# One exponential, product and store for a pair of heads, with accumulators, residual rows and the sample tile moved in a Mamba-2 and latent-attention step

## The chip, the cores and the metric

The kernel runs on one core of a Trainium2 chip. A core has four compute engines that this text calls by their names in the profile: PE (TensorE, the matrix unit), DVE (VectorE), ACT (ScalarE) and POOL (GpSimd). SP (SyncE) computes nothing and issues transfers. Each engine runs its own list of instructions in order, and engines wait for one another by semaphores. SBUF is the on-chip memory with 128 partitions, PSUM the accumulators that PE writes and DVE and ACT read. Transfers are issued from SP's, ACT's or POOL's queue.

The metric is the device time of one launch in microseconds (us), lower is better. Before the change it is 1969.66 us as the median of three runs (1962.78 to 1971.03).

## The reference

One inference step of two layers: a Mamba-2 layer, then a multi-head latent attention layer (MLA). There are 1024 prompt tokens, and eight sequences of eight sample tokens that attend to 2048 cached positions in pages of 128. All of it is in float32. What the change touches is the MLA layer and the final normalisation:

```python
def latent_partial(q_lat, q_pe, ckv, kpe, mask):
    s = (jnp.einsum('bqhc,bkc->bhqk', q_lat, ckv.astype(F32))
         + jnp.einsum('bqhr,bkr->bhqk', q_pe.astype(F32), kpe.astype(F32))) * MLA_SCALE
    if mask is not None:
        s = jnp.where(mask, s, NEG_INF)
    m = jnp.max(s, axis=-1)
    p = jnp.exp(s - m[..., None])
    return m, jnp.sum(p, axis=-1), jnp.einsum('bhqk,bkc->bhqc', p, ckv.astype(F32))
...
def latent_out(l, acc, w_uv):
    return jnp.einsum('bhqc,chv->bqhv', acc / l[..., None], w_uv.astype(F32))
...
def mla_sample_attn(q_nope, q_pe, ckv, kpe, pool_ckv, pool_kpe, layer, page_table, w_uk, w_uv):
...
    stats = latent_partial(q_lat, q_pe, ckv, kpe, causal)
    def page_step(carry, pt):
        page = latent_partial(q_lat, q_pe, pool_ckv[layer, pt], pool_kpe[layer, pt], None)
        return merge_partial(carry, page), None
    (_, l, acc), _ = lax.scan(page_step, stats, page_table.T)
    return latent_out(l, acc, w_uv)

def mla_output(o, gate, w_out):
    b, t = o.shape[:2]
    gated = o.reshape(b, t, MLA_WIDTH) * jax.nn.silu(gate.astype(F32))
    return jnp.einsum('bte,ed->btd', gated.astype(gate.dtype), w_out)
...
        hp = hp + out_p.astype(hp.dtype)
        hs = hs + out_s.astype(hs.dtype)
    y_prompt = rms_norm(hp, final_norm_w)
    y_sample = rms_norm(hs, final_norm_w)
```

There are 16 heads with 64 output columns each, the latent rows have 256 columns, and the model width is 1024.

## The kernel before

**Precision.** A float32 product is made of three matmuls on rounded halves: each operand is split into a high part (`split`, line 128, a copy on ACT) and a low part (line 129, a subtraction on DVE or POOL), and high x high, high x low and low x high are added up in PSUM.

**Stages.** The Mamba-2 layer takes the first half of the time. The MLA layer (`layer_mla`, line 2427) then projects, and runs the prompt's 16 heads one after the other (`mla_heads`, line 1932). The sample's attention over the cached pages is begun within the last two heads and goes on behind them (`mla_sample`, line 2314), with the prompt's output projection laid between its steps.

**Order.** In heads 0 to 13 PE and POOL run in the order of the program text, and a scheduler sorts the other engines' instructions. From head 14 on (`sm.begin`) all engines run in the order of the text.

**A prompt head.** Twelve steps, four for the first 512 queries (qc=0) and eight for the second (qc=1), one for each block of 128 keys. `hd.qk` issues three score matmuls, on the diagonal a fourth for the mask, two exponentials on ACT (th, line 1873, and P, line 1874), and their difference tl (line 1876) on POOL, or on DVE for each fourth block. `hd.pv` runs three steps later: three matmuls into the accumulator `o` (lines 1901 to 1903, one PSUM buffer); at the same time it loads the next gates. Units of work for the coming heads stand between the steps: maxima (`maxpass`, with the matmul nmp on line 1845 that waits for DVE's nm, line 1842), projections, and from head 14 the sample's.

**A head's end.** Behind the last block of a (head, qc), ACT takes the logarithm of the row sums (line 1912), DVE multiplies output and gate into `og` (line 1913), and ACT turns the logarithm into a reciprocal (line 1914). Three steps later, `close` (line 1916) multiplies the two on POOL (line 1917) and stores them to `og_d` in DRAM (line 1918), by SP's queue, and from head 14 by POOL's. Head h uses partitions 64j to 64j+63 with j = h mod 2, so each of the 32 pieces has 64 partitions x 512.

**The sample's start.** `sm.begin` at the start of head 14 makes `nk96`, the new tokens' rotary keys in three parts, with four DVE operations (lines 2051 to 2054). `sm.prefetch` is run as four units of head 14, the first two close together. Each loads a page group by an indirect transfer from POOL (line 2105); the second also transposes `nk96` on PE (line 2071, nkp) and copies it back (line 2072).

**The sample's steps.** `flow` (line 2269) goes over 32 items, four page groups for each of eight sequences. Step n transposes and splits the latent rows of item n+1 (key casts on line 2188, subtractions on 2190), computes the scores of item n, its running maximum (line 2122), and the exponential P (line 2132), and turns P by transposes (pt, line 2219) one step later to multiply it with the latent rows (o). When a sequence has its four items, `turn_acc` (line 2244) transposes its accumulator on PE (act, line 2250) and copies it into accT on DVE (line 2251). In the program before it runs in the step with n mod 4 = 1, right behind `first_acc`, which copies the next sequence's first accumulator on ACT (ac, line 2170).

**The output projection.** `MlaOut.pieces` (line 2346) handles tiles of 128 tokens in four pieces of 12 matmuls each (line 99 in `mm_tok`), one piece for each step of `flow` from step 5 on. At a tile's start the previous tile is closed, the residual rows h are loaded (line 2372), and the next tile's og is loaded. Behind each half of 512 columns DVE adds the product to h (line 2387); behind half 0 the next tile's og is split; behind half 1 ACT squares both halves and sums them (line 2402). The squares' scratch tile has the tag of the og tile, with one buffer for both. `close` (line 2403) makes the scale with two small DVE operations and a power on POOL (line 2407), and scales both halves (line 2414) and stores each (line 2417).

**The tail.** When the items are done, a string says what comes next: p is a piece of the prompt's last tile, a is `turn_acc` of sequence 7, f is `finish` (for eight pairs of heads two matmuls, lo, line 2259, and two DVE products with the gates into gs, line 2266) and starts the sample's output tile, s is a piece of that tile. The sample tile of 64 tokens stores its rows from two queues (lines 2419 and 2420).

```python
TAIL = "papfpssssspp"
```

Of the kernel before, what the change touches and what calls it, by code (L numbers as in the profile page):

```python
# [17 lines left out]
D = 1024  # L18
# [56 lines left out]
    return nc.sync  # L75


TAIL = "papfpssssspp"
PB1 = {"tr": 2, "pj": 2, "cb": 1, "y": 1, "pv": 1, "st": 1}
PB2 = {"tr": 3, "pj": 2, "y": 3}  # L80
PB = dict(PB1)
# [1527 lines left out]
class Heads:  # L1609
# [55 lines left out]
    def open(self, st, right, psum):  # L1665
        k, tc, nc, I = self.k, self.k.tc, self.k.nc, self.k.I
        self.psum = psum
        top = right.enter_context(open_pool(tc, name="kq3", bufs=1, side="right"))
        self.add_k(top, 2)
        self.add_q(top, 2)  # L1670
        sp = self.sp = st.enter_context(open_pool(tc, name="sp3", bufs=1, side="right"))
        self.add_k(sp, 3)
        for a, b in self.kT:
            nc.gpsimd.memset(a[96:98].bitcast(F32), 1.0)
            nc.gpsimd.memset(b[96:98].bitcast(F32), 0.0)
        self.add_v(sp, 1)
        self.load_mask()
        self.load_q(1)
        self.load_gates(0, 0)

    def load_gates(self, h, qc):
        k, pj = self.k, slice(64 * (h % 2), 64 * (h % 2) + 64)
# [203 lines left out]
    def pv(self, h, qc, jb, th, tl):  # L1886
# [20 lines left out]
        pl = slice(64 - 64 * j, 128 - 64 * j)  # L1907
        cs = slice(512 * qc, 512 * qc + 512)
        gt = self.gt
        og = sp.tile([128, 512], F32, tag="og", name=f"og{h}{qc}", bufs=2)  # L1910
        rl = sp.tile([128, 512], F32, tag="rl", name=f"rl{h}_{qc}", bufs=2)
        nc.scalar.activation(rl[pj], po[pl], AF.Ln)
        nc.vector.tensor_tensor(og[pj], po[pj], gt[pj], op=ALU.mult)
        nc.scalar.activation(rl[pj], rl[pj], AF.Exp, scale=-1.0)

        def close():
            nc.gpsimd.tensor_tensor(og[pj], og[pj], rl[pj], op=ALU.mult)
            (nc.gpsimd if h >= MH - 2 else nc.sync).dma_start(k.og_d[pr, pj, cs], og[pj])
        return close


# [109 lines left out]
class Sample:  # L2031
# [8 lines left out]
    def begin(self, st, hd):  # L2040
        k, nc = self.k, self.k.nc
        self.psum, self.out, self.tags = hd.psum, None, {"tr": ("sc", HB[1]), "sc4": ("sc", HB[1]), "on": ("sc", HB[1])}
        sp = self.ep = self.sp = st.enter_context(open_pool(k.tc, name="ep4", bufs=1))
        pp = st.enter_context(open_pool(k.tc, name="pre4", bufs=1))
        self.w5 = dict(zip(WORD, ([pp.tile([128, D], F32R, name=f"w5p{x}") for x in "hl"], hd.kT[2], hd.qT[2], hd.kT[0])))
        self.smk = sp.tile([128, NT], F32, name="smk")
        nc.sync.dma_start(self.smk, k.I["c_smask"])
        self.load_cn(0)
        nk96 = sp.tile([64, 96], F32, name="nk96")
        rnd = sp.tile([64, 32], F32R, name="nkr")  # L2050
        nc.vector.tensor_copy(rnd, k.nkp)
        nc.vector.tensor_copy(nk96[:, 0:32], rnd.bitcast(F32))
        nc.vector.tensor_tensor(nk96[:, 32:64], k.nkp, rnd.bitcast(F32), op=ALU.subtract)
        nc.vector.tensor_copy(nk96[:, 64:96], rnd.bitcast(F32))
        self.nks, self.nk96 = sp.tile([96, 64], F32R, name="nks"), nk96

    def pt(self, tag, name):
        tag, bufs = self.tags[tag]
# [4 lines left out]
        self.k.nc.sync.dma_start(self.cn, self.k.cs_d[b * NT : b * NT + NT])  # L2063

    def prefetch(self):
        nc = self.k.nc
        for n in range(PRE):
            if n == 1:
                self.load_tk(0)
                p = self.pt("tr", "nkp4")  # L2070
                nc.tensor.transpose(p[:96, :64], self.nk96, self.k.ident[:64, :64])
                nc.vector.tensor_copy(self.nks, p[:96, :64])
                load_halves(self.k, self.w5[WORD[0]], WORD[0])
            self.load(n)
            yield
# [174 lines left out]
            nc.tensor.transpose(pt[:, c * 128 : c * 128 + 128], ac[:, c * 128 : c * 128 + 128], k.ident)  # L2250
        nc.vector.tensor_copy(self.accT[:, :, b], pt[:, :256].rearrange("p (c e) -> p c e", c=2))

    def finish(self):
        k, nc, sp, I = self.k, self.k.nc, self.sp, self.k.I
        gs = self.gs
        for pr in range(8):
            p = self.pt("tr", f"lo{pr}")
            for c in range(2):
                nc.tensor.matmul(p[:, :128].rearrange("p (b e) -> p b e", b=NB),
# [9 lines left out]
    def flow(self):  # L2269
        k, N = self.k, len(self.items)  # L2270
        for n in range(-1, N + 1):
# [8 lines left out]
            if t:  # L2280
                self.turn(n + 1, 1)
                yield
            if n % 4 == 1 and n > 4:
                self.turn_acc(n // 4 - 1)
            if n % 4 == 3 and t:
                self.first_scores(n // 4 + 1)
# [27 lines left out]
def mla_sample(k, sm, st):  # L2314
# [8 lines left out]
    for x in TAIL:  # L2323
        if x == "a":
            sm.turn_acc(NB - 1)
        elif x == "f":
            last = out.pieces((8,), sm.finish())
        else:
            next(last if x == "s" else fill, None)
    drain(fill)  # L2330
# [3 lines left out]
class MlaOut:  # L2334
# [11 lines left out]
    def pieces(self, tiles, src=None):  # L2346
        k, nc, sp, ws = self.k, self.k.nc, self.sp, self.ws

        def load(i):
# [4 lines left out]
            if i < 8:  # L2354
                g = sp.tile([128, 8, 128], F32, tag="og5", name=f"og5{i}", bufs=1)
                nc.sync.dma_start(g, k.og_d[:, :, t0 : t0 + m].rearrange("b p t -> p b t"))
            return oh[:, :, :m], oh[:, :, 64:] if m == 64 else ol, g, oh

        queue = [load(tiles[0])]
        if tiles[0] == 0:  # L2360
# [5 lines left out]
        for n, i in enumerate(tiles):  # L2366
            t0, m = TILES[i]
            if close:
                close()
            oh, ol, _, o2 = queue.pop(0)  # L2370
            h = sp.tile([128, D], F32, tag="h5", name=f"h5{i}", bufs=3)
            nc.sync.dma_start(h[:m], k.h_d[t0 : t0 + m])
            if n + 1 < len(tiles):
                queue.append(load(tiles[n + 1]))
            ss = sp.tile([128, 4], F32, tag="ss5", name=f"ss5{i}", bufs=2)
# [3 lines left out]
            for hf, c in enumerate(cs):  # L2379
# [15 lines left out]
                if hf == 0:  # L2395
                    if n + 1 < len(tiles):
                        split(k, *queue[0][:3])
                if c.stop < D:
                    yield
            if not src:  # L2400
                for hf, c in enumerate(cs):
                    nc.scalar.activation(junk[:, c], h[:m, c], AF.Square, accum_out=ss[:m, hf : hf + 1])
            def close(m=m, h=h, ss=ss, O=O, cs=cs):
                r = ss[:m, 3:4]
                nc.vector.tensor_tensor(r, ss[:m, 0:1], ss[:m, len(cs) - 1 : len(cs)], op=ALU.add)
# [124 lines left out]
```

## Time and profile before

| what | number |
|---|---|
| median of three runs | 1969.66 us (1962.78, 1969.66, 1971.03) |
| the profiled execution | 1961.5 us, span 1959.7 us |
| mean clock granted to PE | 0.987 of full speed |
| instructions | 33894 |
| heads stage, first to last product with the reciprocal | 1361.7 to 1692.9 us |
| last matmul begins | 1949.73 us |
| DMA, whole span | 223.79 MB, mean 114 GB/s |

The span runs from the first to the last recorded instruction of one execution, and the execution's own time has 1.8 us around it. The profile gives each engine's busy time; TensorE's granted clock, as a share of full speed, for any window; the waits, named by the waiting tile with its line, and by what released it; and the chain of work that ended last. A row of the timeline has the start, the duration, the engine, the line, the operation with its output and inputs, and in brackets the idle time of the engine before it with what ended it. The lines themselves stand in the prediction.

### The profile page before, as it was taken

What the parts mean: (1) busy time and instruction counts of PE and PEld (TensorE: products, weight loads), DVE (VectorE), ACT (ScalarE), POOL (GpSimd) and SP (SyncE); (2) the same over time, 40 slices, a digit from 0 to 9 for tenths busy, and PEclk for the clock granted to TensorE, in tenths of its full rate; (3) what the DMA queues carried; (4) which work ended last, traced back from release to release, by engine and by line L of the source; (5) the groups of instructions that cost most, each with busy time, mean ns of one, the idle gap of its engine ahead of it and who ended that gap; (6) DMA issues with size and microseconds to landing.
All of it is one profiled execution on the core that took longest, in us unless ns stands there. A gap on an engine that the chain in (4) does not pass through costs nothing.

```text
span 1959.7 us, 33894 instructions
## 1 busy us (share of the span) xinstructions
PE 1887.0 (96%) x11953; PEld 1732.7 (88%) x11953; DVE 1165.8 (59%) x2566; ACT 1105.8 (56%) x2605; POOL 789.0 (40%) x1094
## 2 busy tenths in 40 slices
PE   7999999999999999799999999999999999899997
PEld 6999999999999999687787998898888887788886
DVE  5457575757575757544425325476777776656664
ACT  5556666666666666643334424335777776655551
POOL 2037373736363657233000001103564556744540
PEclk9999999999999999899999999999999999999999
DMA  5123333233333332644554772232121112854542
GB/s 152 53 61 92 92 89 93 89 92 89 92 89 91 91 89 80 207 153 158 186 181 133 265 281 78 68 108 71 51 70 41 48 45 85 278 150 132 151 128 66
DMA packets 193936, 223.79 MB, mean 114 GB/s; under 512 B 20284, under 2 KB 155336, under 8 KB 193384
## 3 DMA queue, kind: packets, MB, share of 16 engines
q1 hardware_dynamic: 188744, 202.10, 33.9%
q0 software_dynamic: 4944, 19.40, 3.1%
q8 instruction: 95, 1.56, 0.3%
q14 instruction: 73, 0.60, 0.1%
q10 hardware_dynamic: 80, 0.13, 0.0%
HBM read 159.89 MB, written 61.54 MB: 113 GB/s over the span
## 4 chain that ended last, share of the span: by engine, by line
PE 87%; DMA 5%; DVE 3%; ACT 3%; issue 1%; SPq 0%; POOL 0%; ACTq 0%; DVEq 0%; POOLq 0%
PE pj L87 24%; PE pj L99 9%; PE pq L99 6%; PE p L99 4%; PE poa L99 4%; PE pob L99 4%; PE py L863 3%; PE sc L87 2%; PE o L87 2%; PE sc L1830 2%; PE st L1862 2%; PE o L1903 1%; PE st L1863 1%; PE st L1864 1%; PE o L1902 1%; PE o L1901 1%
## 5 line engine op out<-in xcount | busy, mean ns | idle before, releaser
L87 PE MATMUL pj<-xh,wih 128*128 128x384 f32 (+1 forms) x768 | 255.1, 332 | 0.0
L87 PE MATMUL pj<-xh,wil 128*128 128x384 f32 (+1 forms) x768 | 250.8, 327 | 0.0
L87 PE MATMUL pj<-xl,wih 128*128 128x384 f32 (+1 forms) x768 | 250.4, 326 | 0.0
L1876 POOL TENSOR_TENSOR tl<-P,th 128x384 fp32r<-128x384 f32 (+1 forms) x144 | 131.5, 920 | 140.2 <-ACT P L1874 104.7
L129 DVE TENSOR_TENSOR wil<-wraw,wih 128x512 fp32r<-128x512 f32 x92 | 70.4, 765 | 172.6 <-ACT wih L128 172.6
L87 PEld LDWEIGHTS pj<-xh,wih 128*128 128x128 f32 x768 | 144.5, 188 | 0.2
L87 PEld LDWEIGHTS pj<-xl,wih 128*128 128x128 f32 x768 | 144.4, 188 | 0.3
L87 PEld LDWEIGHTS pj<-xh,wil 128*128 128x128 f32 x768 | 144.1, 188 | 0.0
L900 POOL TENSOR_TENSOR y<-y,xD 128x256 f32<-128x256 f32 x64 | 83.9, 1311 | 149.4 <-DVE y L899 138.5
L99 PE MATMUL pj<-wih,xh 128*128 128x256 f32 x504 | 143.3, 288 | 0.0
L99 PE MATMUL pj<-wil,xh 128*128 128x256 f32 (+1 forms) x504 | 139.2, 282 | 0.0
L1873 ACT ACTIVATE th<-st 128x512 fp32r<-128x512 f32 x192 | 94.3, 491 | 69.4 <-PE st L1869 46.7
L2190 POOL TENSOR_TENSOR kvl<-pgr,kvh 128x256 fp32r<-128x256 f32 x128 | 92.2, 748 | 96.3 <-ACT kvh L2188 96.2
L495 DVE SCALAR_TENSOR_TENSOR acc<-raw,vec,acc 128x1112 f32<-128x1112 f32 x84 | 130.5, 1554 | 0.2
L99 PE MATMUL pj<-wih,xl 128*128 128x256 f32 x448 | 126.6, 283 | 0.0
L129 POOL TENSOR_TENSOR xddl<-xdd,xddh 128x256 fp32r<-128x256 f32 x64 | 63.1, 986 | 119.5 <-ACT xddh L128 119.5
L128 ACT CAST Ch<-acc 128x128 fp32r<-128x128 f32 x56 | 16.9, 302 | 153.0 <-PE py L87 153.0
L99 PEld LDWEIGHTS pj<-wih,xh 128*128 128x128 f32 x504 | 96.0, 191 | 0.0
L1874 ACT ACTIVATE P<-st 128x512 f32<-128x512 f32 x192 | 93.4, 486 | 4.3 <-POOL tl L1876 4.0
L99 PEld LDWEIGHTS pj<-wil,xh 128*128 128x128 f32 (+1 forms) x504 | 93.0, 185 | 0.6
L838 ACT ACTIVATE M<-M,tok 128x128 f32<-128x128 f32 (+1 forms) x288 | 90.5, 388 | 1.8 <-DMA M<-acs_d 1.8
L99 PEld LDWEIGHTS pj<-wih,xl 128*128 128x128 f32 x448 | 85.4, 191 | 0.0
(995 smaller groups left out, 6210.4 us busy)
## 6 DMA issues: line engine op xcount, KB each, us to landing
wraw<-in_ssd_w_in SPq DMA_DIRECT2D x92, 256.0 KB
M<-acs_d SPq DMA_DIRECT2D x64, 256.0 KB
y_d<-xD SPq DMA_DIRECT2D x64, 128.0 KB
s<-in_state_ssm SPq DMA_DIRECT2D x32, 256.0 KB
out_s_ssm<-s SPq DMA_DIRECT2D x32, 256.0 KB
wraw<-in_ssd_w_out SPq DMA_DIRECT2D x16, 512.0 KB
q_d<-qt SPq DMA_DIRECT2D x32, 192.0 KB
qp<-q_d SPq DMA_DIRECT2D x8, 768.0 KB
```

The source lines that it names most:

```text
L87: nc.tensor.matmul(out, a, b, start=(i == 0), stop=(i == n - 1))
L99: nc.tensor.matmul(o, a, b, start=(j == 0), stop=(j == len(ops) - 1))
L129: (eng or nc.vector).tensor_tensor(lo, src, hi.bitcast(F32), op=ALU.subtract)
L495: nc.vector.scalar_tensor_tensor(acc, self.raw[bi][:, j : j + n], k.convw[j][:, blk : blk + 1], acc, op0=ALU.mult, op1=ALU.add)
L838: nc.scalar.activation(M[:m, h, :m], M[:m, h, :m], AF.Relu, bias=c.tk[:, 0, 4 * g + h : 4 * g + h + 1], scale=-1.0)
L863: nc.tensor.matmul(py[:m, h * 64 : h * 64 + 64], c.M[:m, h, :m], c.xdt[:m, h * 64 : h * 64 + 64], start=True, stop=True)
L900: nc.gpsimd.tensor_tensor(y[:m], y[:m], c.xD[:m], op=ALU.add)
L1830: nc.tensor.matmul(ps[:, :n], qh[:96, 128 * i : 128 * i + 128], kh[:96, 512 * c : 512 * c + n], start=True, stop=True)
L1873: nc.scalar.activation(th[:, :n], ps[:, :n], AF.Exp, scale=SCALE)
L1874: nc.scalar.activation(P[:, :n], ps[:, :n], AF.Exp, scale=SCALE)
L1876: eng.tensor_tensor(tl[:, :n], P[:, :n], th[:, :n].bitcast(F32), op=ALU.subtract)
L2190: nc.gpsimd.tensor_tensor(rl[:, r], raw[:, r], rh[:, r].bitcast(F32), op=ALU.subtract)
```

## The change

1. The pair's tiles. `og` and `rl` are four fixed tiles of 128 x 512, one of each for a qc. Each head still takes its own logarithm and gate product on its 64 partitions. The even head then ends; the odd head does one exponential, and three steps later one product and one store over both halves. The store goes by POOL's queue for head 15 only.
2. `nk96` is made in the first unit of `prefetch` instead of in `begin`.
3. `turn_acc` runs in the step with n mod 4 = 2 instead of 1.
4. The residual rows h are loaded in `load`, along with the og of the same tile, so a tile ahead.
5. Each half's square follows its own half: half 0's right behind the split of the next tile's og, half 1's at the end.
6. `finish` takes a list of pairs and is called twice, f for pairs 0 to 3 and g for pairs 4 to 7 with the start of the sample's tile, and in the tail all prompt pieces come ahead of the sample's.

```diff
--- before.py
+++ after.py
@@ -75,7 +75,7 @@
     return nc.sync
 
 
-TAIL = "papfpssssspp"
+TAIL = "papfpgpssss"
 PB1 = {"tr": 2, "pj": 2, "cb": 1, "y": 1, "pv": 1, "st": 1}
 PB2 = {"tr": 3, "pj": 2, "y": 3}
 PB = dict(PB1)
@@ -1677,6 +1677,7 @@
         self.load_mask()
         self.load_q(1)
         self.load_gates(0, 0)
+        self.ogs, self.rls = ([sp.tile([128, 512], F32, name=f"{x}{qc}") for qc in range(2)] for x in ("og", "rl"))
 
     def load_gates(self, h, qc):
         k, pj = self.k, slice(64 * (h % 2), 64 * (h % 2) + 64)
@@ -1907,15 +1908,16 @@
         pl = slice(64 - 64 * j, 128 - 64 * j)
         cs = slice(512 * qc, 512 * qc + 512)
         gt = self.gt
-        og = sp.tile([128, 512], F32, tag="og", name=f"og{h}{qc}", bufs=2)
-        rl = sp.tile([128, 512], F32, tag="rl", name=f"rl{h}_{qc}", bufs=2)
+        og, rl = self.ogs[qc], self.rls[qc]
         nc.scalar.activation(rl[pj], po[pl], AF.Ln)
         nc.vector.tensor_tensor(og[pj], po[pj], gt[pj], op=ALU.mult)
-        nc.scalar.activation(rl[pj], rl[pj], AF.Exp, scale=-1.0)
+        if j == 0:
+            return
+        nc.scalar.activation(rl, rl, AF.Exp, scale=-1.0)
 
         def close():
-            nc.gpsimd.tensor_tensor(og[pj], og[pj], rl[pj], op=ALU.mult)
-            (nc.gpsimd if h >= MH - 2 else nc.sync).dma_start(k.og_d[pr, pj, cs], og[pj])
+            nc.gpsimd.tensor_tensor(og, og, rl, op=ALU.mult)
+            (nc.gpsimd if h == MH - 1 else nc.sync).dma_start(k.og_d[pr, :, cs], og)
         return close
 
 
@@ -2046,13 +2048,9 @@
         self.smk = sp.tile([128, NT], F32, name="smk")
         nc.sync.dma_start(self.smk, k.I["c_smask"])
         self.load_cn(0)
-        nk96 = sp.tile([64, 96], F32, name="nk96")
-        rnd = sp.tile([64, 32], F32R, name="nkr")
-        nc.vector.tensor_copy(rnd, k.nkp)
-        nc.vector.tensor_copy(nk96[:, 0:32], rnd.bitcast(F32))
-        nc.vector.tensor_tensor(nk96[:, 32:64], k.nkp, rnd.bitcast(F32), op=ALU.subtract)
-        nc.vector.tensor_copy(nk96[:, 64:96], rnd.bitcast(F32))
-        self.nks, self.nk96 = sp.tile([96, 64], F32R, name="nks"), nk96
+        self.nk96 = sp.tile([64, 96], F32, name="nk96")
+        self.nkr = sp.tile([64, 32], F32R, name="nkr")
+        self.nks = sp.tile([96, 64], F32R, name="nks")
 
     def pt(self, tag, name):
         tag, bufs = self.tags[tag]
@@ -2063,8 +2061,13 @@
         self.k.nc.sync.dma_start(self.cn, self.k.cs_d[b * NT : b * NT + NT])
 
     def prefetch(self):
-        nc = self.k.nc
+        nc, nkp = self.k.nc, self.k.nkp
         for n in range(PRE):
+            if n == 0:
+                nc.vector.tensor_copy(self.nkr, nkp)
+                for j in (0, 2):
+                    nc.vector.tensor_copy(self.nk96[:, 32 * j : 32 * j + 32], self.nkr.bitcast(F32))
+                nc.vector.tensor_tensor(self.nk96[:, 32:64], nkp, self.nkr.bitcast(F32), op=ALU.subtract)
             if n == 1:
                 self.load_tk(0)
                 p = self.pt("tr", "nkp4")
@@ -2250,10 +2253,10 @@
             nc.tensor.transpose(pt[:, c * 128 : c * 128 + 128], ac[:, c * 128 : c * 128 + 128], k.ident)
         nc.vector.tensor_copy(self.accT[:, :, b], pt[:, :256].rearrange("p (c e) -> p c e", c=2))
 
-    def finish(self):
+    def finish(self, pairs):
         k, nc, sp, I = self.k, self.k.nc, self.sp, self.k.I
         gs = self.gs
-        for pr in range(8):
+        for pr in pairs:
             p = self.pt("tr", f"lo{pr}")
             for c in range(2):
                 nc.tensor.matmul(p[:, :128].rearrange("p (b e) -> p b e", b=NB),
@@ -2280,7 +2283,7 @@
             if t:
                 self.turn(n + 1, 1)
                 yield
-            if n % 4 == 1 and n > 4:
+            if n % 4 == 2 and n > 4:
                 self.turn_acc(n // 4 - 1)
             if n % 4 == 3 and t:
                 self.first_scores(n // 4 + 1)
@@ -2324,7 +2327,9 @@
         if x == "a":
             sm.turn_acc(NB - 1)
         elif x == "f":
-            last = out.pieces((8,), sm.finish())
+            sm.finish(range(4))
+        elif x == "g":
+            last = out.pieces((8,), sm.finish(range(4, 8)))
         else:
             next(last if x == "s" else fill, None)
     drain(fill)
@@ -2354,7 +2359,9 @@
             if i < 8:
                 g = sp.tile([128, 8, 128], F32, tag="og5", name=f"og5{i}", bufs=1)
                 nc.sync.dma_start(g, k.og_d[:, :, t0 : t0 + m].rearrange("b p t -> p b t"))
-            return oh[:, :, :m], oh[:, :, 64:] if m == 64 else ol, g, oh
+            h = sp.tile([128, D], F32, tag="h5", name=f"h5{i}", bufs=3)
+            nc.sync.dma_start(h[:m], k.h_d[t0 : t0 + m])
+            return oh[:, :, :m], oh[:, :, 64:] if m == 64 else ol, g, oh, h
 
         queue = [load(tiles[0])]
         if tiles[0] == 0:
@@ -2367,9 +2374,7 @@
             t0, m = TILES[i]
             if close:
                 close()
-            oh, ol, _, o2 = queue.pop(0)
-            h = sp.tile([128, D], F32, tag="h5", name=f"h5{i}", bufs=3)
-            nc.sync.dma_start(h[:m], k.h_d[t0 : t0 + m])
+            oh, ol, _, o2, h = queue.pop(0)
             if n + 1 < len(tiles):
                 queue.append(load(tiles[n + 1]))
             ss = sp.tile([128, 4], F32, tag="ss5", name=f"ss5{i}", bufs=2)
@@ -2395,11 +2400,10 @@
                 if hf == 0:
                     if n + 1 < len(tiles):
                         split(k, *queue[0][:3])
+                if not src:
+                    nc.scalar.activation(junk[:, c], h[:m, c], AF.Square, accum_out=ss[:m, hf : hf + 1])
                 if c.stop < D:
                     yield
-            if not src:
-                for hf, c in enumerate(cs):
-                    nc.scalar.activation(junk[:, c], h[:m, c], AF.Square, accum_out=ss[:m, hf : hf + 1])
             def close(m=m, h=h, ss=ss, O=O, cs=cs):
                 r = ss[:m, 3:4]
                 nc.vector.tensor_tensor(r, ss[:m, 0:1], ss[:m, len(cs) - 1 : len(cs)], op=ALU.add)
```

## The prediction

> **What bounds the kernel now.** First the page: busy times, then the shares of the chain of waits that ended last.
>
> ```profile
> PE 1887.0 (96%) x11953; PEld 1732.7 (88%) x11953; DVE 1165.8 (59%) x2566; ACT 1105.8 (56%) x2605; POOL 789.0 (40%) x1094
> PE 87%; DMA 5%; DVE 3%; ACT 3%; issue 1%; SPq 0%; POOL 0%; ACTq 0%; DVEq 0%; POOLq 0%
> ```
>
> TensorE is busy 96% of the span and carries 87% of the chain, so work taken off ACT, POOL or SP is worth something only where TensorE waits for it. Before 1340 us the change touches nothing. Next comes the view of TensorE's waits from there on, asked in four stretches; columns: total us, count, longest.
>
> ```profile
> PE nmp L1845 <- DVE nm L1842: 2.7, 4, 1.0
> PE o L1903 <- POOL tl L1876: 3.8, 1, 3.8
> PE act L2250 <- ACT ac L2170: 4.1, 7, 1.6
> PE lo L2259 <- DVE gs L2266: 3.1, 1, 3.1
> ```
>
> These are the waits that the change can reach. Last the view by windows: a steady stretch of the heads, then the stretches around three of these waits.
>
> ```profile
> core 0: us, PE busy (x) PEld busy (x) DVE busy (x) ACT busy (x) POOL busy (x), PEclk, DMA share, GB/s
> 1600.00:1640.00 40.00, 39.01 (x227) 33.99 (x226) 31.43 (x82) 31.20 (x69) 23.03 (x27) 1.00 0.12 28
> 1652.80:1656.60 3.80, 0.05 (x1) 0.00 (x0) 0.42 (x1) 0.01 (x1) 2.56 (x3) 0.80 0.07 18
> 1656.60:1662.10 5.50, 5.49 (x17) 4.71 (x18) 1.41 (x4) 1.59 (x5) 5.17 (x6) 0.52 0.28 63
> 1709.80:1713.20 3.40, 3.35 (x9) 2.77 (x10) 2.53 (x5) 0.47 (x1) 2.71 (x3) 0.51 1.03 412
> 1930.30:1933.40 3.10, 0.02 (x1) 0.00 (x1) 1.13 (x4) 0.00 (x0) 0.00 (x0) 1.00 0.29 91
> 1933.40:1938.40 5.00, 4.97 (x23) 4.42 (x24) 3.72 (x15) 0.62 (x1) 0.00 (x0) 0.66 0.00 0
> ```
>
> The heads run at 39.01 of 40 us with the clock at 1.00: 1 us in 40 can be had there. The long waits cost twice: the wait itself, and a stretch behind it at a clock of 0.51 to 0.66, in which a matmul takes about twice as long.
>
> **Change part by part.** *Exponential, product and store per pair.*
>
> ```profile
> L1914 ACT ACTIVATE rl<-rl x32: 621/629/636, 1358.3 to 1689.4; 64x512 f32<-64x512 f32 x32
> L1917 POOL TENSOR_TENSOR og<-og,rl x32: 1259/1278/1603, 1361.7 to 1692.9; 64x512 f32<-64x512 f32 x32
> ```
>
> (Rows grouped by operation: shortest, mean and longest in ns, first and last start.) No row shows these operations on 128 partitions; DVE's products take 0.69 for 64x512 and for 128x512 alike (L1913 and L2387 below), so I take the same for 128 as for 64; at the other bound, twice, nothing would be saved and nothing lost. So 16 x 0.63 = 10 us leave ACT, 16 x 1.28 = 20 us leave POOL, and 16 stores leave the queues (the rest are twice as large). Over 330 us of heads all of it lies behind TensorE's 39 of 40: 0. If that cover were gone it would be a gain, not a loss. What counts is one place, on POOL (timeline: start, us, engine, line, operation; in brackets the idle time before and what ended it):
>
> ```profile
> 1646.66 1.00 POOL L2105 DMA_INDIRECT pgr<-in_cache_ckv,ptidx  x1 [0.30 <-PE o L1902]
> ...
> 1653.96 1.26 POOL L1917 TENSOR_TENSOR og<-og,rl 64x512 f32<-64x512 f32 x1 [4.96 <-DMA pgr<-in_cache_ckv,ptidx]
> ```
>
> The product of head 13 sat 4.96 us behind the landing of page loads that it doesn't use. The subtraction queued behind it on POOL is the one that TensorE waits for (3.8). In the program built from the change, the product waits for the store that last read its tile, for DVE and for ACT, all long done. It then starts at about 1649.0, ends at 1650.3, and the subtraction (1.30) at 1651.6, before TensorE asks at 1652.8. Gain: the 3.8 us, and the half clock behind it, where 5.5 us at 0.52 hold work worth 5.5 x 0.52 = 2.9, so 2.6. I take -6.2; the bounds are 0, if something else holds POOL there, and -6.4.
>
> Two later stalls should shrink, as POOL has a product less in front of them:
>
> ```profile
> 1685.26 0.39 PE L87 MATMUL o<-kvh,pTl 128*128 128x256 f32 x1 [0.94 <-DVE pTl L129]
> ...
> 1695.27 0.66 PE L2219 MATMUL pt<-ident,P 128*128 128x128 f32 x4 [1.40 <-ACT P L2132]
> ```
>
> From 0 to all but 0.6 of their 2.3: I take -0.8.
>
> *The new page's key rows (nk96) moved to prefetch.* Four small DVE operations leave the start of head 14, where they stood ahead of the maximum that a matmul awaits (nmp, longest 1.0). The three other waits of this kind make (2.7 - 1.0) / 3 = 0.6 each and stay, so the gain lies between 0.4 and 1.0; I take -0.7. The operations now stand on DVE behind head 13's gate product, directly ahead of their transposes, whose place on TensorE hasn't moved:
>
> ```profile
> 1636.07 0.85 DVE L2051 CAST nkr<-nkp 64x32 fp32r<-64x32 f32 x1
> 1637.65 0.17 DVE L2053 TENSOR_TENSOR nk<-nkp,nkr 64x32 f32<-64x32 f32 x1
> ...
> 1642.67 0.59 ACT L1912 ACTIVATE rl<-o 64x512 f32<-64x512 f32 x1
> 1642.90 0.26 PE L2071 MATMUL nkp<-ident,nk 64*96 64x64 f32 x1
> 1643.30 0.69 DVE L1913 TENSOR_TENSOR og<-o,gt 64x512 f32<-64x512 f32 x1 [0.26 <-ACT rl L1912]
> ```
>
> TensorE comes to the transpose at 1642.90; the gate product, which waits for the logarithm, ends at 1643.99; four operations at 0.17 make it 1644.7, at 0.85 each 1647.4. So this is a new wait of 1.8 to 4.5 us, with all scores of head 14 behind it in TensorE's queue. POOL is idle then, so the short ones are nearer: +2.0. Waits of 0.94 and 1.40 us had full clock behind them, the one of 1.6 (act, below) had 0.51: a stretch like 1709.80 to 1713.20 costs 3.4 x 0.49 = 1.7, and I count somewhat under half, +0.7. [...]
>
> *Accumulator turned a step later.*
>
> ```profile
> 1709.85 0.69 PE L2250 MATMUL act<-ident,ac 128*128 128x128 f32 x2 [1.56 <-ACT ac L2170]
> 1742.38 0.44 PE L2250 MATMUL act<-ident,ac 128*128 128x128 f32 x2 [0.43 <-ACT ac L2170]
> ```
>
> In the program before, the transpose shares a PSUM buffer with the next batch's first accumulator and waits for ACT's copy issued just ahead. A page step later that copy is some 7 us old; what is left is DVE's copy out of the step before, done by then. 1.56 + 6 x 0.43 = 4.1, and the half clock from 1709.8, 3.4 x 0.49 = 1.7, of which I take 1.4: -5.5 (at least -2.6, if a wait of 0.2 stays in each and the clock still drops; at most -5.8).
>
> *Squares.* Rows of the timeline in the page loop; that of pt is from the chain of waits.
>
> ```profile
> 1723.15 1.03 ACT L128 CAST oh<-og 128x1024 fp32r<-128x1024 f32 x1
> 1724.22 1.22 DVE L129 TENSOR_TENSOR ol<-og,oh 128x1024 fp32r<-128x1024 f32 x1 [0.20 <-ACT oh L128]
> 1729.87 0.69 ACT L2132 ACTIVATE P<-sc,nm 128x512 f32<-128x512 f32 x1 [0.65 <-DVE nm L2125]
> 1733.06 0.44 PE pt L2219 x4
> 1738.33 0.63 ACT L2402 ACTIVATE sq<-h 128x512 f32<-128x512 f32 x1
> 1743.45 0.41 DVE L2251 COPY accT<-act 128x256 f32<-128x256 f32 x1
> ```
>
> Half 0's Square now follows the split of the next tile's outputs. Its scratch tile shares a buffer with the rows that DVE subtracts there, so ACT stands 1.22 for it and 0.63 for the Square, 1.85 in all, once a tile, with the exponential P and the key cast queued behind. P is ready at 1730.56 and its transposes run at 1733.06: 2.5 us of slack, so 0. At the tile's end one Square less: 0.
>
> *Residual rows a tile ahead.* TensorE has no wait on h before the tail, SP issues it behind the next tile's outputs instead of ahead of them, and neither is waited for there: 0.
>
> *Tail.* The sample tile goes last, and its second half of pairs finishes later, so the wait of 3.1 (lo for gs) goes, and with it the half clock at 0.66: 5.0 x 0.34 = 1.7; together -4.8. What is late instead (the first row is from the chain of waits):
>
> ```profile
> 1927.03 5.08 DMA h<-h_d
> ...
> 1937.38 0.69 DVE L129 TENSOR_TENSOR oh<-gs,oh 128x512 fp32r<-128x512 f32 x1 [0.73 <-ACT oh L128]
> 1939.78 0.40 PE L99 MATMUL p<-w5ph,oh 128*128 128x512 f32 x1
> 1943.64 0.68 DVE L2387 TENSOR_TENSOR h<-h,p 64x512 f32<-64x512 f32 x1 [5.56 <-PE p L99]
> 1951.90 0.58 ACTq L2419 DMA_DIRECT2D out_y_sample<-h  x1
> 1951.92 0.69 DVE L2387 TENSOR_TENSOR h<-h,p 128x512 f32<-128x512 f32 x1
> 1954.40 0.55 POOL L2407 TENSOR_TENSOR ss<-ss,nhalf 128x1 f32<-128x1 f32 x1 [3.29 <-DVE ss L2406]
> 1954.99 1.41 DVE L2414 SCALAR_TENSOR_TENSOR h<-h,ss,fw 128x512 f32<-128x512 f32 x2 [0.75 <-POOL ss L2407]
> ```
>
> In DVE's order the split of the sample's outputs (0.69) now stands behind the whole close of tile 7: add 0.69, Square 0.63, the power on POOL 0.55, two scalings 1.41, with the hand-overs 4.7 from the last prompt matmul (about 1937.75) to the sample's first (1942.45). That is +4.7. The half clock behind it costs 1.5 to 2.6. The sample's own chain from its first add to its store's issue, 1951.90 - 1943.64 = 8.3 us, ends the kernel in place of a prompt tile's shorter one. Its h load, queued behind tile 7's two stores, is issued at about 1942.4 and with 5.08 lands 1 us before its use. I get the last store issued at 1956.8 and the end at 1960.0, against 1959.7: +0.3 net (-0.6 to +1.3).
>
> Sum: -6.2 - 0.8 - 0.7 + 2.0 + 0.7 - 5.5 + 0.3 = -10.2. The span of 1959.7 becomes 1949.5, and the profiled 1961.5 (1.8 around the span) 1951.3. The median of the runs shown is 8.2 above that execution, while the lowest run, 1962.78, agrees with it; I set the sum on the mean of all four, 1966.2: **1956**.
>
> **Rivals.** *R1, the gain of the long wait is given back.* From 1692 on the DMA engines are full (share 1.03 in the row at 1709.80): weights and pages then land no earlier however soon POOL is done, and the 6.2 returns as waits for data. For it: that row. Against it: TensorE's waits of 1.4 and 1.6 there name ACT, not a transfer. -4 to -5: 1962.
>
> *R2, slower: ACT's wait in the split.* If P is later than its slack of 2.5, each of the seven tiles pays. It decides from 2.5 us of lateness: the 1.85 above, and whatever DVE's subtraction is late because the accumulator's copy (0.41) now falls into the same step. With the slack used up, 7 x (2.1 + 0.4) = 17 us, and 3 more if half clock follows some: -10 + 17 = +7, up to +10, 1973 to 1976. For it: every n mod 4 = 2 step gains both. Against it: 1.85 + 0.41 is still under 2.5.
>
> *R3, a larger gain.* The nkp wait has no half clock behind it, both later stalls vanish and the tail's wait is shorter than 4.7: -14, 1952. For it: full clock behind 1.40.
>
> *R4, the change doesn't do what it says:* the product still waits for POOL's loads: -10.2 + 6.2 = -4, the same time as R1 and counted with it.
>
> **How the numbers follow.** Forecast 0.54, R3 0.16, R1 with R4 0.20, R2 0.10. Some 0.5% (9.8 us) is what a measurement can tell from nothing. The forecast's spread, 3 us either way, puts 0.31 of its 0.54 beyond it; with R3 0.16 and 0.02 of R1, faster is 0.49. Of R2, 0.08 lies beyond +0.5%. Same is 0.43. The range: all gains at their bounds make -14, 1952, and the runs shown lie 4 us about their middle, so 1947 below; above, R1's -4.5 on the median shown, 1969.7, is 1965, and nkp's upper bound with its half clock adds 3.5 to 4: 1969. R2 is left out, and the two gains of -6.2 and -5.5 failing together. The forecast's own range is 1951 to 1961.
>
> **What would show it.** No PE wait for POOL's tl near 1653; one for nk of 1.8 to 2.3 at the nkp transpose; no act waits; P's slack above 0 in the steps that follow a split; one PE wait of about 4.7 ahead of the sample's first matmul, named after DVE's split. A new wait at pt in several tiles would make it wrong, as would a wait of over 4 us for nk.

## The result and the profile after

The changed kernel takes 0.9961 of the time of the one before (95% interval 0.9943 to 0.9979): medians 1958.45 us and 1964.30 us over eight runs each. 0.39% of 1964 is 7.7 us, between 4.1 and 11.2. The forecast was 10.2 us less, 1956 us, with a range of its own from 1951 to 1961: the sign is right, and the size is right within the interval. The experiments below show that the gains and losses also stand about where they were forecast, but that some of them come from other edits than the prediction credited.

The profiled execution of the changed kernel took 1958.8 us, span 1957.0, and so lies 2.7 us under that of the kernel before, less than the medians do. First the page's busy times:

```profile
PE 1887.2 (96%) x11953; PEld 1733.8 (89%) x11953; DVE 1163.1 (59%) x2566; ACT 1095.9 (56%) x2589; POOL 767.4 (39%) x1076
```

ACT lost 9.9 us and POOL 21.6, as counted, and TensorE's share stands at 96%. The prediction assumed that the exponential and the product take as long on 128 partitions as on 64 (0.629 and 1.278 us); the rows of the changed kernel show it (shortest, mean and longest in ns):

```profile
L1916 ACT ACTIVATE rl<-rl x16: 629/633/636, 1378.0 to 1690.6; 128x512 f32<-128x512 f32 x16
L1919 POOL TENSOR_TENSOR og<-og,rl x16: 1276/1286/1301, 1384.7 to 1692.8; 128x512 f32<-128x512 f32 x16
```

Next TensorE's waits in the stretches asked of the kernel before (total us, count, longest):

```profile
PE nmp L1846 <- DVE nm L1843: 1.7, 3, 0.6
...
PE nkp L2074 <- DVE nk L2070: 1.9, 1, 1.9
...
PE p L99 <- DMA w5h<-w_d: 1.0, 1, 1.0
PE p L99 <- DMA w5l<-w_d: 0.9, 1, 0.9
...
PE p L99 <- DVE oh L129: 4.7, 1, 4.7
```

The waits for POOL's tl (3.8), of act for ac (4.1) and of lo for gs (3.1) are gone, and nmp's is down by 1.0. The two forecast waits are there in the forecast size: nkp 1.9 and the sample's first matmul 4.7. Not forecast in this place are the two waits for weights, 1.9 together. The windows behind the two new waits:

```profile
core 0: us, PE busy (x) PEld busy (x) DVE busy (x) ACT busy (x) POOL busy (x), PEclk, DMA share, GB/s
112.00:114.00 2.00, 0.00 (x0) 0.00 (x0) 0.72 (x3) 1.97 (x7) 0.61 (x1) 0.98 0.00 0
114.00:117.40 3.40, 3.24 (x11) 3.24 (x12) 1.30 (x3) 3.37 (x7) 0.16 (x1) 0.51 0.12 24
1645.10:1647.00 1.90, 0.00 (x1) 0.00 (x0) 1.62 (x7) 1.26 (x4) 1.02 (x2) 0.87 0.23 64
1647.00:1653.30 6.30, 6.26 (x17) 5.18 (x18) 2.10 (x6) 1.45 (x3) 2.13 (x2) 0.50 0.85 292
1933.40:1938.20 4.80, 0.06 (x2) 0.04 (x1) 3.01 (x6) 1.23 (x3) 0.55 (x1) 0.84 0.12 44
1938.20:1943.50 5.30, 5.30 (x13) 3.39 (x14) 0.00 (x0) 0.00 (x0) 0.00 (x0) 0.50 0.34 109
```

Behind nkp's 1.9 us the clock was at 0.50 for 6.3 us, by the missing half an estimated 3.1; behind the 4.7 in the tail for 5.3 us, 2.6. The first two rows are a part of why the profiles lie closer together than the medians: at 114 us, in a part whose instructions the change doesn't touch, this execution ran 3.4 us at 0.51, and the profiled execution of before at 1.00 (114.00 to 117.40 us). With matching instructions set side by side, the changed kernel is 1.7 us behind from there on. At 1400 us it is 4.3 behind, after a wait of 1.6 for P and another 3.4 us at half clock (0.50 from 1383.70 to 1387.10). At 1662 us it is 0.5 us behind, is 3.3 us ahead at 1713, level again at 1733 behind the weights, 4.2 ahead at 1930, and 1.7 ahead at the last matmul.

### The profile page after: what moved, and what is told of

The parts are those of the page before. It is cut to its first block, busy times and chain, and to the rows that moved or that the text cites. A ratio compares the mean times of both kernels' runs of the same rounds, so it can differ in the third digit from the quotient of the medians.

```text
span 1957.0 us, 33747 instructions
## 1 busy us (share of the span) xinstructions
PE 1887.2 (96%) x11953; PEld 1733.8 (89%) x11953; DVE 1163.1 (59%) x2566; ACT 1095.9 (56%) x2589; POOL 767.4 (39%) x1076
## 3 DMA queue, kind: packets, MB, share of 16 engines
q8 instruction: 95, 1.56, 0.3%
```

## The experiments

All kernels were timed against the kernel before on the same chips. A "us" for a ratio takes 1964 us as the whole.

| kernel | ratio to before | 95% interval |
|---|---|---|
| changed kernel, again | 0.9967 | 0.9955 to 0.9979 |
| changed, weights on other memory (a_w5) | 0.9958 | 0.9943 to 0.9972 |
| changed, nkp a unit later (a_nk) | 0.9948 | 0.9934 to 0.9962 |
| changed, sample's split earlier (a_tail) | 0.9919 | 0.9899 to 0.9939 |
| changed, these three together (a_all) | 0.9906 | 0.9886 to 0.9926 |
| changed, squares undone (a_sq) | 0.9967 | 0.9954 to 0.9980 |
| changed, residual rows undone (a_hback) | 1.0027 | 1.0011 to 1.0042 |
| before + turn_acc (b_act) | 0.9999 | 0.9985 to 1.0013 |
| before + turn_acc + residual rows (b_acth) | 0.9953 | 0.9935 to 0.9970 |
| before + pair's tiles (b_pair) | 0.9970 | 0.9956 to 0.9984 |
| before + tail (b_tail) | 1.0025 | 1.0008 to 1.0041 |
| before + nk96 (b_nk) | 1.0005 | 0.9992 to 1.0018 |

**The changed kernel again.** The same program, to see what repeats.

> The changed kernel once more, to see which parts of its profile repeat. [...]

The span was 1953.0, 4 us under the first, with a mean granted clock of 0.988 against 0.985. Windows of this second execution, at nkp and behind it:

```profile
1645.00:1648.30 3.30, 1.83 (x8) 1.51 (x9) 1.57 (x6) 0.83 (x3) 1.85 (x4) 1.00 0.43 120
1648.30:1651.70 3.40, 3.40 (x13) 3.04 (x12) 2.04 (x6) 1.90 (x4) 0.80 (x1) 0.51 0.94 316
1651.70:1655.10 3.40, 3.40 (x18) 2.83 (x17) 2.08 (x5) 2.80 (x6) 3.05 (x3) 0.99 0.87 316
```

The waits came again (nk 1.9, split 4.7; of the two for weights one, w5l, of 1.2), but the half clock behind nkp lasted 3.4 us (0.51) instead of 6.3 (0.50). What follows from it for reading two profiles stands in the last section.

**Weights on other memory.** In the changed kernel SP's first load of a weight word waits 3.9 us for the last store of og1, whose memory it takes.

```diff
-        for kk in WORD[4:]:
+        for kk in WORD[:3:-1]:
             self.ws[kk] = ...
```

> The changed kernel with the tiles of the last four weight words allocated in reverse, so that the word loaded first no longer lies on the memory of og1 and rl1, and the word loaded last does. Theory (the first load waits for the last store of og1 to land, and SP's whole queue behind it): SP issues the first w5h load near 1693.5 instead of 1700.1, TensorE's two waits for w5h and w5l of 0.9 and 1.0 us go, and so does what else the late key loads cost: 2 to 3 us less than the changed kernel. Rival (the DMA engines are full from 1690 to 1720 and the weights land late whatever the order): SP's issue moves, but the waits stay within 0.5 us and the time doesn't change.

SP issued the first w5h at 1691.6 instead of 1700.1 and the last at 1707.0 instead of 1710.3. TensorE is 3.8 us ahead of the first execution of the changed kernel there, so the first load went 4.8 us earlier against TensorE and the last one no earlier. One wait of 0.7 for w5l remained, and the waits of P at pt rose from 0.7 to 2.3 (a_nk, without this edit, has 2.0). 0.9958 against 0.9967: the intervals overlap, and neither theory is settled. The kernel b_acth, which keeps the old og tiles, has the same two waits:

```profile
PE p L99 <- DMA w5h<-w_d: 1.8, 1, 1.8
PE pt L2219 <- ACT P L2132: 0.9, 2, 0.5
PE p L99 <- DMA w5l<-w_d: 0.9, 1, 0.9
```

So the memory of og1 is not their only cause. In both kernels the first tile's residual rows go out ahead of these weights; but a_hback, where they go out behind them, has the waits too (1.6 and 0.8). In the changed kernel the DMA engines are at a share of 0.9 in the 10 us from 1690 and from 1700, and of 1.0 from 1710; in the kernel before they are at 1.02, 1.06 and 1.08 in the same stretches, without such a wait. The cause stays open.

**nkp a unit later.**

```diff
             if n == 1:
                 self.load_tk(0)
+                load_halves(self.k, self.w5[WORD[0]], WORD[0])
+            if n == 2:
                 p = self.pt("tr", "nkp4")
...
                 nc.vector.tensor_copy(self.nks, p[:96, :64])
-                load_halves(self.k, self.w5[WORD[0]], WORD[0])
```

> The changed kernel with the nk96 transposes and their copy in the third unit of prefetch instead of the second, some steps behind the four DVE operations. Theory (the wait of 1.9 us is only the distance between gate product and transpose on a busy DVE): the wait goes, and the half clock behind it where it had one: 2 to 4.5 us less. Rival (it is exchanged): the later place has a wait of its own for DVE or for a free PSUM buffer, of 1 us or more, and the time stays within 1 us.

No wait for nk remained. 0.9967 to 0.9948 is 3.7 us less, the theory's size, though the intervals overlap a little.

**The sample's split ahead of tile 7's last piece.**

```diff
-TAIL = "papfpgpssss"
+TAIL = "papfpgspssss"
...
         split(k, *queue[0][:3])
-        if tiles[0] == 0:
+        if tiles[0] == 0 or src is not None:
             yield
```

> The changed kernel with the sample's og split (and its residual load) issued ahead of tile 7's last piece instead of behind it. Theory (the wait of 4.7 us ahead of the sample's first matmul is DVE's queue: the split stands behind tile 7's close): the wait goes, and with it most of the half clock of 6.8 us in the sample's 20 matmuls; the last matmul ends 5 to 8 us earlier, and the end comes 5 to 8 us earlier too. Rival (the end is set by the two closes and stores on DVE, SP and ACT): the last matmul comes earlier, but the end moves by less than 3 us, as tile 7's close then stands among the sample's own DVE operations.

TensorE has no wait left in the tail, and the sample's first matmul starts beside tile 7's close. 0.9967 to 0.9919 is 9.4 us, with intervals that don't touch: the theory, and by its middle somewhat more than the 5 to 8 us expected. DVE's rows of this kernel show what became of tile 7's close:

```profile
1937.03 0.69 DVE L129 TENSOR_TENSOR oh<-gs,oh 128x512 fp32r<-128x512 f32 x1 [0.73 <-ACT oh L128]
1938.54 0.69 DVE L2392 TENSOR_TENSOR h<-h,p 128x512 f32<-128x512 f32 x1 [0.81 <-PE p L99]
...
1941.09 1.42 DVE L2418 SCALAR_TENSOR_TENSOR h<-h,ss,fw 128x512 f32<-128x512 f32 x2 [0.72 <-POOL ss L2411]
1942.42 0.67 DVE L2392 TENSOR_TENSOR h<-h,p 64x512 f32<-64x512 f32 x1
```

The split stands ahead of tile 7's add now, and the close runs beside the sample's matmuls; the sample's first add follows the scalings without idle time.

**All three edits together.**

> The changed kernel with all three edits: weight words allocated in reverse, nkp in the third unit of prefetch, the sample's split ahead of tile 7's last piece. If the three causes are separate, the gains add up: 9 to 15 us less than the changed kernel, 0.988 to 0.991 of the kernel before. Rival: a wait that one edit removes is only covered by another's, and the sum is under 6 us.

0.9906 of the kernel before, median 1945.68 us: by the ratios 12.0 us under the changed kernel run again, within the theory's 9 to 15. It is the fastest kernel here.

**turn_acc alone, on the kernel before.**

```diff
-            if n % 4 == 1 and n > 4:
+            if n % 4 == 2 and n > 4:
                 self.turn_acc(n // 4 - 1)
```

> The kernel before with one edit: turn_acc in the step with n mod 4 = 2. Prediction's step: -2.6 to -5.8 us, likeliest -4 to -5.5: all seven act waits (4.1 us together) gone, no new wait at pt. Rival: ACT's extra lateness in these steps (split, Square at the tile's end) turns up as waits at pt, and less than 2 us is left.

0.9999: no change that the times show, and at most 2.9 us less. The seven act waits are gone and waits at pt have come, where the kernel before has 0.9 (waits of TensorE, 1700 to 1925):

```profile
PE pt L2219 <- ACT P L2132: 2.6, 5, 1.0
```

The rival's sign, but the trace names another cause. One of these steps, on ACT:

```profile
1818.84 1.05 ACT L128 CAST oh<-og 128x1024 fp32r<-128x1024 f32 x1 [3.65 <-DMA og<-og_d]
1819.79 1.04 ACT L2188 CAST kvh<-pgr 128x1024 fp32r<-128x1024 f32 x1
```

ACT stood 3.65 us for the og of the next tile to land, with the cast of the next keys queued behind it. That transfer is the next thing late. TensorE was 2.3 us ahead of the kernel before at 1805, but the og landed when it had there (the cast starts at 1818.84 against 1818.74), and at 1827 the lead was 0.5. That is not the whole account, though: at 1900 the lead is 2.3 again, and 1.7 us of new pt waits stand against 4.1 us of act waits gone. What hides the rest in the times isn't shown.

**turn_acc with the residual rows a tile ahead, on the kernel before.** The edit of b_act, and lines 2371 and 2372 moved into `load`, as in the change.

> The kernel before with two edits, turn_acc in the step with n mod 4 = 2 and the residual rows a tile ahead. turn_acc alone gave 0.9999 of the kernel before: its seven waits of 4.1 us went and waits at pt came. Theory (og landing late took the gain): with h out of og's way the waits at pt stay below 1 us, the tail's wait of lo for gs shrinks as tile 7's residual rows are there, and the time falls by 4 to 9 us. Rival (ACT's own queue in these steps took the gain): still within 2 us of the kernel before, but for the tail's 3 us.

0.9953, 9.2 us less, with the pt waits at 0.9 in all; and no wait of TensorE is left in the old tail: the 3.1 us of lo for gs are gone without any change to the tail. This row of the kernel before, on DVE, says why:

```profile
1932.23 0.69 DVE L2387 TENSOR_TENSOR h<-h,p 128x512 f32<-128x512 f32 x1 [5.77 <-DMA h<-h_d]
```

The products that make gs stood behind this add, and the add stood 5.77 us for tile 7's residual rows. The gain over b_act stands in the tail: from the first lo to the end are 26.3 us instead of 32.5, while the page loop isn't shorter (the table behind the experiments).

**The residual rows back in their place, in the changed kernel.** The h load ahead of the next tile's og again; all else as changed.

> The changed kernel with the residual rows loaded at their own tile's start again, ahead of the next tile's og on SP. Theory (h's 512 KB stand in front of og on the queues, and og's landing is what sets the split): ACT waits longer for og, waits at pt come, and in the tail DVE waits for tile 7's residual rows: 3 to 6 us more than the changed kernel. Prediction's step: no wait in the page loop; in the tail only a wait of 2 to 3 us for h.

1.0027 against 0.9967: 11.8 us more, twice the upper end of what was expected, and slower than the kernel before. ACT's waits for og from 1720 to 1935 (total us, count, longest), in the kernel before:

```profile
ACT oh L128 <- DMA og<-og_d: 10.7, 6, 2.9
```

In the changed kernel:

```profile
ACT oh L128 <- DMA og<-og_d: 5.1, 3, 3.8
```

And with the residual rows back in their place:

```profile
ACT oh L128 <- DMA og<-og_d: 20.8, 7, 8.2
```

In the traces the page loop is some 12 us longer than the changed kernel's and the tail 2, where DVE waits for tile 7's residual rows again. One tile of the loop, from SP's, ACT's and TensorE's timelines:

```profile
1815.67 0.43 SPq L2377 DMA_DIRECT2D h<-h_d  x1
1816.19 0.62 SPq L2361 DMA_DIRECT2D og<-og_d  x1
...
1824.57 1.05 ACT L128 CAST oh<-og 128x1024 fp32r<-128x1024 f32 x1 [2.91 <-DMA og<-og_d]
1826.91 0.63 ACT L2404 ACTIVATE sq<-h 128x512 f32<-128x512 f32 x1 [1.29 <-DVE ol L129]
1827.54 1.03 ACT L2191 CAST kvh<-pgr 128x1024 fp32r<-128x1024 f32 x1
...
1833.28 0.66 PE L2222 MATMUL pt<-ident,P 128*128 128x128 f32 x4 [0.96 <-ACT P L2135]
```

From og's issue to the cast that needs it are 8.4 us here, behind h's 512 KB. In the changed kernel the same tile has 6.05, and ACT doesn't wait for it:

```profile
1808.77 0.41 SPq L2361 DMA_DIRECT2D og<-og_d  x1
1809.23 0.77 SPq L2363 DMA_DIRECT2D h<-h_d  x1
...
1814.82 1.05 ACT L128 CAST oh<-og 128x1024 fp32r<-128x1024 f32 x1
```

Behind the late cast stand the Square, the key cast and P, and P arrives late: 6.1 us of pt waits over eight of them, where the changed kernel has 0.7. The late og alone doesn't do it. b_act has the residual rows ahead of og too, and ACT waits 16.6 us for og there, yet it has 2.6 us of pt waits and no longer loop than b_acth. What a_hback has beside it is the Square, which stands 1.29 us for DVE and runs 0.63 between the two casts: from the start of the og cast to that of the key cast are 2.97 us here and 0.95 in the rows of b_act. No kernel with the residual rows and the squares both undone was run, so that the two cost this only together is read from four kernels' traces, not tested.

**The squares undone, in the changed kernel.** Both at the tile's end again.

> The changed kernel with both squares of a prompt tile back at its end. Theory (the next tile's og load waits for the last Square, since the scratch tile has its one buffer, and lands just in time): og lands 0.6 to 0.8 us later in each tile, ACT's split and the key cast behind it are later, and waits of P at pt come in the steps with n mod 4 = 2: 1 to 4 us more than the changed kernel. Rival (prediction's step: the squares cost nothing either way; what lets og land early is the residual rows moved out of its way): within 1 us of the changed kernel.

0.9967, the ratio of the changed kernel run again: the rival, and the prediction's step. ACT's waits for og are 5.2 as against 5.1. This holds for squares with the residual rows a tile ahead.

**The pair's tiles alone, on the kernel before.** The edits of the first part of the change.

> The kernel before with one edit: four fixed og and rl tiles, one exponential, product and store for a pair. Theory: the 3.8 us wait for POOL's tl near 1653 goes with its half clock (-3.8 to -6.4), and the first w5 load behind the last store costs 2 to 3 us of it near 1720: -2 to -4 in all. Rival 1 (prediction's R4): the product still waits for the page loads, nothing gained there. Rival 2 (the memory's reuse costs nothing): -5 to -7.

0.9970, 5.9 us less. No wait for POOL's tl in its profile, and none for weights, though SP's first w5h waits 1.9 us for the store here too. Nearer rival 2 than the theory; rival 1 is out.

**The tail alone, on the kernel before.** `finish` in two halves and TAIL = "papfpgpssss".

> The kernel before with one edit: finish in two halves and the sample's tile last. Prediction's step: the 3.1 us wait of lo for gs goes, a wait of some 4.7 us ahead of the sample's first matmul comes, and the end moves by -0.6 to +1.3 us. In this kernel the sample's residual rows are loaded at the tile's own start, behind tile 7's two stores, as the change has it too. Rival: the residual rows land late and hold the sample's first add, +2 us or more.

1.0025, 4.9 us more. Both waits of TensorE are there, the one that was forecast and one for the residual rows:

```profile
PE p L99 <- DVE oh L129: 4.7, 1, 4.7
PE p L99 <- DVE h L2389: 2.1, 1, 2.1
```

The rows late are tile 7's, on which DVE's add waits as in the old tail, not the sample's, as the rival had it:

```profile
1933.43 0.69 DVE L2389 TENSOR_TENSOR h<-h,p 128x512 f32<-128x512 f32 x1 [5.17 <-DMA h<-h_d]
```

**nk96 alone, on the kernel before.**

> The kernel before with one edit: nk96 made in the first unit of prefetch. Prediction's step: nmp's wait of 1.0 us falls to 0.3 or less, a wait of 1.8 to 2.3 us comes at the nkp transposes, some half clock behind it: +1 to +3.5 us together. Rival: as the wait for POOL's tl near 1653 follows and ends with the landing of a page load, TensorE's lateness is absorbed there, and the time stays within 1 us.

1.0005 (0.9992 to 1.0018). The nkp wait is 1.7, nmp's is down by 1.0, and the wait for POOL's tl that follows shrank from 3.8 to 2.6, as the rival says; the interval holds both.

**By stretch.** The profiled executions, divided at two matmuls that all kernels have: the loop from the start of the last st (the prompt's last scores) to that of the first lo, and the tail from there to the end of the span. Each figure is of one execution, with its own half clock: in the tail 5.0 us at 0.66 in the kernel before, and 5.3 us at 0.50 in the first execution of the changed kernel.

| kernels | loop, us | tail, us |
|---|---|---|
| before, b_pair, b_nk | 243.8 to 244.6 | 31.4 to 31.5 |
| b_tail | 242.9 | 35.8 |
| b_act | 240.7 | 32.5 |
| b_acth | 240.9 | 26.3 |
| changed (twice), a_sq, a_w5, a_nk | 238.1 to 242.3 | 31.8 to 33.1 |
| a_hback | 252.0 | 34.9 |
| a_tail, a_all | 239.6 to 239.9 | 25.6 |

## Why the prediction was right in sum, and where it credited the wrong edit

- **Product for a pair, -7.0.** Right: 5.9 measured. The product no longer waits for page loads, and the 3.8 us wait went, and with it the half clock (5.5 us at 0.52 before; 1.00 from 1653.4 to 1700 in the changed kernel). It is gone in all nine profiles with the pair's tiles and stands at 2.6 to 4.8 us in the five without. The -0.8 of it for the two later stalls did not come: 2.3 us for pTl and P there became 1.7, and 0.9 for a load came beside them.
- **nk96, +2.0 net of nmp's -0.7 and the clock's +0.7.** The sizes of the waits were right: 1.9 at nkp, 1.0 off at nmp. The clock was mis-sized: "somewhat under half" of 1.7 us, where the two executions lost an estimated 3.1 and 1.7 (6.3 us at 0.50, 3.4 at 0.51), and removing the wait is worth 3.7 us. On the kernel before, part of it was absorbed by the stall behind it.
- **turn_acc, -5.5.** Too much. The act waits went as forecast ("what is left is DVE's copy out of the step before, done by then"), but nothing was asked about what is late next, the og transfer, and 1.7 us of waits at pt came. By itself the edit shows nothing in the times (-2.9 to +2.6); in the trace the loop is 2 to 4 us shorter.
- **Residual rows, 0: the step that was wrong.** "SP issues it behind the next tile's outputs instead of ahead of them, and neither is waited for there." TensorE doesn't wait for them, but ACT waits 10.7 us for og in six steps of the kernel before. The tile that the prediction shows (the cast at 1723.15) is the one of seven in which it doesn't. And the old tail's wait hung on tile 7's residual rows. Loaded a tile ahead they are worth some 6 us in the tail beside turn_acc alone; put back into the changed kernel they cost 11.8, most of it in the loop, where the squares now stand too. The views that would have told it are the waits of ACT and DVE, not of TensorE.
- **Tail, +0.3.** The number was near: 31.4 us before, 31.8 to 33.1 with the change. The new wait of 4.7 was right to a tenth, and the half clock behind it within the range: an estimated 2.6 (5.3 us at 0.50), then 1.7, where in the second execution, from 1935.08 us, a 128x512 matmul took 0.63 us for 3.4 us and 0.39 behind that. Wrong was the edit credited with -4.8: that wait of lo for gs was rooted in tile 7's late residual rows, and the load a tile ahead removes it without the new order. The new order by itself is a loss, 4.9 us on the kernel before, and 9.4 us come back when the split is taken out from behind the close.
- **Squares, 0.** Right as the change was built: 0.9967 with and without. But it holds by the residual rows, which the prediction put at nothing as well: with them late, a_hback's loop is 12 us longer, and its rows show the Square in the way. That the change moved both is luck for the forecast.
- **The sum.** Measured apart: -5.9 for the pair, +1.0 for nk96, -9.2 for turn_acc with the residual rows, +4.9 for the tail: -9.2. The whole gives -7.7, and -6.5 in the second set of runs. The four have intervals of 2.6 to 3.4 us either way, so these times show no interaction. The traces do: the wait of lo for gs goes in b_acth and goes in b_tail, so the sum counts it twice. The forecast's -10.2 came near since its terms by place were near (a loop shorter by 4 to 5 us instead of 5.5, a tail longer by 1 instead of 0.3), whichever edit they were put down to.
- **R1** came in part: 1.9 us of waits for weights in the full DMA stretch. What sets their landing stayed open; the edit of their memory moved the time by less than its interval.
- **R2** named the right mechanism, with P late behind the split, and a price of the right order: 2.5 us a tile by its text, 1.3 on average over the last six tiles of a_hback, which ends slower than before. It needs what the prediction counted, ACT's stand for DVE and the Square, and what it didn't, an og that lands late; the residual rows' move kept it away.
- **R3 and R4.** nkp's wait had half clock behind it in both executions of the changed kernel (6.3 us at 0.50, 3.4 at 0.51), where R3 wanted none. R4 didn't come: the product no longer waits for POOL's loads.

## What to carry to other kernels

When a wait of the bounding engine is removed, ask of each other engine in that step what it waits for, and how late that is. Two delays in one engine's queue can each be harmless and cost much together, as the late og and the Square seem to do on ACT here; so an edit found free is free only beside the others it was measured with. A wait names the last link alone; follow it back (lo for gs, gs behind an add, the add for a load) before crediting a reordering with its removal. A first operation of the last tile shouldn't be queued behind the close of the tile before it.

## What the runs showed of the hardware

The granted clock behind the same wait was not the same in each execution. At 114 us, in work that the change doesn't touch, TensorE waited 3.06 us for cbm in the profile of before and 3.07 in that of the changed kernel; from 114.00 to 117.40 us the clock was then 1.00 in the one and 0.51 in the other. Behind the nkp wait of 1.9 us it was 0.50 for 6.3 us in the first execution of the changed kernel and 0.51 for 3.4 us in the second. In the profile of before, the waits of 0.94 and 1.40 us had 1.00 behind them (1680 to 1700 us), and the one of 1.56 for ac had 0.51 (1709.80 to 1713.20). What decides it isn't shown; what a wait of 1.5 to 2 us costs in clock here is an estimate. In the changed kernel, at 0.50, a 128x512 matmul took 0.63 us and the next began 0.43 behind its start (1648.32 us); at 1.00 it took 0.40 and 0.23 (1653.47 us).

In 29 runs of the kernel before, the fastest, 1955.37 us, had a mean granted clock of 0.990 and the slowest, 1968.00 us, 0.983; in a_tail's six, 1943.00 us went with 0.991 and 1956.60 us with 0.985. So runs of one kernel lie 13 us apart, more than the change's 7.7. Two single profiles of this kernel therefore can't be compared by their spans, and the spans only over several runs. Waits that hang on an engine's own queue came alike: nkp's 1.9 us in six profiles (the changed kernel's two, a_w5, a_tail, a_sq, a_hback), the split's 4.7 in seven (these but a_tail, and a_nk and b_tail), the act waits' 4.1 in four (before, b_pair, b_tail, b_nk). One wait that ends with a transfer did not: that of st for kTh is absent in a_sq and 2.4 us in a_tail, two kernels that differ only behind it.
